# Issuing a stage's modulation weights from GpSimd, two contraction tiles in one transfer, with the bias added as a column

## The chip, the cores and the metric

The kernel runs on one core of a Trainium2 chip. The metric is the device time of one launch in microseconds, as the median of several runs. The engines are TensorE (PE, with its weight loads PEld), VectorE (DVE), ScalarE (ACT), GpSimd (POOL) and SyncE (SP, which only issues transfers). Each engine works through its own instructions in order and waits on semaphores for the others.

## The reference

A backbone of two layers works on 256 latent tokens and 256 context tokens of width 2048. Each layer first turns the conditioning vector into six modulation rows of 2048 values (shift, scale and gate of the mixer, then shift, scale and gate of the feed-forward part):

```python
sh1, sc1, g1, sh2, sc2, g2 = jnp.split(jax.nn.silu(c) @ ada_w[l] + ada_b[l], 6, axis=-1)
h = modulate(x_lat, norm_mix[l], sh1, sc1)
...
y, yc = even_mixer(h, hc, ...)        # layer 0: gated DeltaNet heads beside neighbourhood attention
y = shortconv_mixer(h, ...)           # layer 1
...
x_lat = x_lat + g1[:, None, :] * y
x_lat = x_lat + g2[:, None, :] * swiglu(modulate(x_lat, norm_ffn[l], sh2, sc2), ...)
```

Here `modulate` is an RMS norm with a learned gain, times one plus the scale, plus the shift. All values are float32. `ada_w[l]` is 2048 x 12288, so each modulation row of 2048 values costs a read of 16 MB of weights.

## The kernel before

**Matrix products.** The large products split each weight tile into a high and a low part (`split_w`: ScalarE writes `whi`, VectorE writes `wlo` at L250) and each takes three matmuls. The weights come as 512 KB tiles `raw` that SyncE issues at L236, with four buffers in the mixer's part. `fm_stream` (matmuls at L348) leaves features on the partitions, `tm_stream` (L303, L304, L308, L320) leaves tokens there.

**The mixer of layer 0.** After the projections of the DeltaNet keys, queries and values come, in this order, the attention's keys and values (`C_KB`, `C_VB`, two halves each), its queries in two halves with the attention heads between them (`na_scores`, `na_values`), the gate `C_ZA`, and the output product `ev_w_out` in two halves. The recurrence of the DeltaNet heads is laid between the steps of these streams (`plan`). Near the end of the value projection seven loads of 512 KB bring back the latent half of the inputs (`hC`, L1276); these are the only transfers that GpSimd issues. GpSimd also clears the tiles `xd` and `xdT` (L1053, L1054) and copies blocks (L1006). In the attention each head loads its position bias `bq` (L1307) and its keys and values from SyncE.

**The modulation of the mixer's stage.** Three modulation rows of layer 0 are needed only after the mixer: the gate of the mixer (`seg` 2, kept as a row) and the shift and scale of the feed-forward part (`seg` 3 and 4, kept as columns). They are not made by matmuls but by VectorE, in `ada_mixer`, which cuts them into 12 blocks of 512 columns. For a block, VectorE clears an accumulator `acc` of 128 x 512 (L430), SyncE loads the 512 bias values into its first partition (L431), and for each of the 16 contraction tiles `k` SyncE loads a tile `araw` of 128 x 512 values, 256 KB (L433), and VectorE multiplies it with the column `cT[:, k]` and adds it to the accumulator (`total`, L438). `close` then sums `acc` over the partitions with four small matmuls against ones (L445) and `ada_done` writes the four resulting columns: with the gain for a scale (L358), as a copy otherwise (L360).

There are six buffers `araw` (`AB`) and the loads run six tiles ahead (`AHEAD`): right after `total(i)` the load of tile i + 6 is issued, into the buffer that this sum has just freed. A block is closed `LAG` steps after its last sum. `Pump` draws the 192 steps along with the steps of the streams: 1.6 per step in the attention's keys and values, 0.6 in its queries, 2.0 in the gate and the output product; what is left is drawn at the end of the output product. A sum is tied behind the last written `wlo` (`last_lo`).

**The order.** The program is written in a certain order, and a planner that simulates the engines (`schedule_with_timeline_sim=True`) places each instruction on its engine's queue. Where SyncE's and GpSimd's transfers stand in their queues is so decided ahead of the run; at run time each queue keeps its order.

**Start.** At the start ScalarE loads the biases of the first two modulation rows as `brow`, 32 rows of 128, and a transpose makes the columns `bT` of them (L661). A tile `pad_e` of 48 columns keeps the layout of the memory.

Of the kernel before, what the change touches and what calls it, by code (L numbers as in the profile page):

```python
# [23 lines left out]
F32 = mybir.dt.float32  # L24
F32R = mybir.dt.float32r
AF = mybir.ActivationFunctionType
OP = mybir.AluOpType
AX = mybir.AxisListType

D = 2048  # L30
# [15 lines left out]
AB = 6  # L46
AHEAD = 6
# [65 lines left out]
def body(tc, x, c, ctx, c_ctx, ada_w, ada_b, norm_mix, norm_ffn, ffn_w_gate, ffn_w_up, ffn_w_down,  # L113
# [3 lines left out]
    PE, ACT, DVE, POOL, SP = nc.tensor, nc.scalar, nc.vector, nc.gpsimd, nc.sync  # L117
# [23 lines left out]
    def pool(name, bufs=1, stack=root, **kw):  # L141
        if kw.get("space") is not bass.MemoryType.DRAM:
            kw.setdefault("reuse_waits", "tile")
        p = stack.enter_context(tc.tile_pool(name=name, bufs=bufs, **kw))
        return p if "space" in kw else Rows(p)
# [3 lines left out]
    epool = pool("even")  # L149
# [11 lines left out]
    def smt():  # L161
        small.append(small.pop(0))
        return small[0].tile([128, 512], F32, name="sm", tag="sm")
# [11 lines left out]
    def acopy(dst, src):  # L175
        ACT.activation(dst, src, AF.Copy)  # L176
# [8 lines left out]
    def C(n):  # L185
        o, w = CO[n]
        return cs[:, o:o + w]
# [5 lines left out]
    def transpose(dst, src):  # L193
        n = src.shape[0]
        return PE.transpose(dst, src, ident[:n, :n])  # L195

    cT = cpool.tile([128, 32], F32, name="cT")
# [4 lines left out]
    shc = {}  # L202
    scc = {}
    gcol = {}
# [147 lines left out]
            yield  # L352


    def ada_done(l, seg, kind, gamma, fs_, p):

        if kind == "sc":
            DVE.scalar_tensor_tensor(scc[l, seg - 1][:, fs_], p, 1.0, gamma[:, fs_], op0=OP.add, op1=OP.mult)  # L358
        else:
            DVE.tensor_copy((shc if kind == "sh" else gcol)[l, seg][:, fs_], p)  # L360
# [3 lines left out]
    def ada_job(pool_, l, seg, kind, gamma=None):  # L364
# [5 lines left out]
        def close(acc, blk):  # L370
            fs_ = slice(blk * 8, (blk + 1) * 8)
            at = pool_.tile([128, 32, 32], F32, name="accT", tag="accT", bufs=1)
            ar = pool_.tile([128, 8, 4], F32, name="accR", tag="accR", bufs=1)
            DVE.transpose(at.rearrange("p b r -> p (b r)"), acc)
            for _ in range(LATER):
                yield
            DVE.tensor_reduce(ar.rearrange("p k b -> p (k b)"), at, axis=AX.X, op=OP.add)
            for _ in range(LATER):
                yield
            p = smt()  # L380
            for b in range(4):
                PE.matmul(p[b * 32:b * 32 + 32, 0:8], C("fold"), ar[:, :, b], start=True, stop=True)
            if kind == "row":
                gc = pool_.tile([128, 8], F32, name="gcol8", tag="gcol8", bufs=1)
                acopy(gc, p[:, 0:8])
                pc = smt()
                transpose(pc[0:8, 0:128], gc)
                g = pool_.tile([16, 128], F32, name="grow", tag="grow", bufs=1)[0:8]
                acopy(g, pc[0:8, 0:128])
                ACT.dma_start(row_d[l, seg][fs_], g)  # L390
            else:
                ada_done(l, seg, kind, gamma, fs_, p[:, 0:8])
# [22 lines left out]
    def ada_mixer(pool_, parts):  # L415


        wr = ada_w[0].rearrange("(k p) n -> p k n", p=128)
        blocks = [(seg, kind, gamma, b) for seg, kind, gamma in parts for b in range(4)]
        accs, raws = {}, {}  # L420

        def load(i):
            n, k = divmod(i, KT)
            if n >= len(blocks):
                return
            seg, b = blocks[n][0], blocks[n][3]
            c0 = seg * D + b * 512
            if not k:
                acc = accs[n] = pool_.tile([128, 512], F32, name="acc", tag="acc", bufs=2)
                DVE.memset(acc, 0.0)  # L430
                SP.dma_start(acc[0:1, :], ada_b[0:1, c0:c0 + 512])  # L431
            raws[i] = pool_.tile([128, 512], F32, name="araw", tag="araw", bufs=AB)
            SP.dma_start(raws[i], wr[:, k, c0:c0 + 512])  # L433

        def total(i):
            n, k = divmod(i, KT)
            with tc.issue_after(last_lo[0]):
                DVE.scalar_tensor_tensor(accs[n], raws.pop(i), cT[:, k:k + 1], accs[n], op0=OP.mult, op1=OP.add)  # L438

        def close(n):  # L440
            seg, kind, gamma, b = blocks[n]
            acc = accs.pop(n)
            p = smt()
            for f in range(4):
                PE.matmul(p[:, f:f + 1], acc[:, f * 128:(f + 1) * 128], ones[:, 0:1], start=True, stop=True)  # L445
            ada_done(0, seg, kind, gamma, slice(b * 4, b * 4 + 4), p[:, 0:4])
            if kind == "row" and b == 3:
                p = smt()
                transpose(p[0:16, 0:128], gcol[0, seg])
                g = pool_.tile([16, 128], F32, name="grow", tag="araw", bufs=AB)  # L450
                DVE.tensor_copy(g, p[0:16, 0:128])
                SP.dma_start(row_d[0, seg], g)

        for i in range(AHEAD):
            load(i)
        N = len(blocks) * KT
        for i in range(N + LAG):
            if i < N:
                total(i)
                load(i + AHEAD)  # L460
            if i >= KT + LAG - 1 and (i - LAG + 1) % KT == 0:
                close((i - LAG + 1) // KT - 1)
            yield
# [77 lines left out]
    sp = pool("start", stack=st, side="right")  # L541
# [15 lines left out]
    p = smt()  # L557
# [7 lines left out]
    ACT.dma_start(vrow[0:32, :], norm_mix.rearrange("l (k p) -> (l k) p", p=128))  # L565
    ACT.dma_start(vrow[32:64, :], norm_ffn.rearrange("l (k p) -> (l k) p", p=128))
    ACT.dma_start(vrow[64:112, :], od_conv.rearrange("o t (k p) -> (o t k) p", p=128))
    brow = sp.tile([32, 128], F32, name="brow")
    bT = sp.tile([128, 32], F32, name="bT")
    ACT.dma_start(brow, ada_b[0:1, 0:4096].rearrange("o (r p) -> (o r) p", p=128))  # L570
    ACT.dma_start(erow, ev_conv.rearrange("o t (k p) -> (o t k) p", p=128))
    ACT.dma_start(cs[:, 128:NCST], cst[:, 128:NCST])
    g_mix = [vecT[:, l * 16:(l + 1) * 16] for l in range(2)]
# [77 lines left out]
    def columns():  # L651

        p = smt()
        transpose(p[:, 0:112], vrow)
        DVE.tensor_copy(vecT, p[:, 0:112])
        p = smt()
        transpose(p[:, 0:120], erow)
        DVE.tensor_copy(evcT, p[:, 0:120])
        p = smt()
        transpose(p[:, 0:32], brow)  # L660
        DVE.tensor_copy(bT, p[:, 0:32])  # L661

    acopy(pick, C("pick"))
    alog = epool.tile([128, 16], F32, name="alog")
    dtb = epool.tile([128, 16], F32, name="dtb")
    gnb = epool.tile([128, 128], F32, name="gnb")


    scale = HD ** -0.5
# [100 lines left out]
    def qa_evac(q):  # L770
# [12 lines left out]
        return head_evac(2, q, 16, done, True)  # L783

    columns()
    with tc.issue_after(token_features()):
        firsts = [split_w(load_w([(wv, C_KA, 512)], 0, 2)), split_w(load_w([(wv, C_KA + 512, 256)], 0, 4))]
# [15 lines left out]
    for b in range(8):  # L803
# [4 lines left out]
        p = smt()  # L808
# [29 lines left out]


    pump = Pump([ada_mixer(adap, [(2, "row", None), (3, "sh", None), (4, "sc", g_ffn[0])])], 1, 1)  # L840

    drive(fm_stream([(wv, C_KA + 768, 256)], ks, [0, 1], lambda f, p: ka[1](f + 2, p)), every=2)
# [28 lines left out]
    eg = epool.tile([128, 3, 2, 4, 8], F32, name="eg")  # L871
    negegc = epool.tile(gsh, F32, name="negegc")
    brest = epool.tile(gsh, F32, name="brest")
    epool.tile([128, 48], F32, name="pad_e")

    def gates():
        w = abp
# [522 lines left out]
    def norm_row(t):  # L1400

        DVE.tensor_reduce(ss2[:, t:t + 1], ssx[:, t, :], axis=AX.X, op=OP.add)
        return rstd(rpool, ss2[:, t:t + 1], [128, 1], 1, D, f"nx{t}")
# [222 lines left out]
    for half in range(2):  # L1626
        c0 = half * 1024
# [7 lines left out]
        for f in range(8):  # L1635
            k = half * 8 + f
            p = smt()
# [25 lines left out]
    for t in range(2):  # L1663
        r = norm_row(t)
# [37 lines left out]
```

## Time and profile before

| | |
|---|---|
| time before, median of 3 runs | 2723.41 us (2722.6 to 2723.89) |
| the profiled execution's own time | 2726.88 us |
| its span, from the first to the last instruction | 2725.1 us |
| transfers moved | 682.71 MB, mean 251 GB/s |
| of these by GpSimd's queue (q0) | 1904 packets, 3.67 MB |
| mean granted clock of TensorE | 0.992 |

The profile is of one execution. Busy times say how long an engine had an instruction in work. A window row gives its length, then for each engine its busy time and its number of instructions, then the granted clock of TensorE as a share of full speed, the mean busy share of the 16 DMA engines and the GB/s that they moved. In a timeline row the last bracket is the idle time of the engine ahead of the instruction and what ended it. Engines marked with q (SPq, POOLq) are the issuing queues of an engine.

### The profile page before, as it was taken

The numbers are of one execution on the slowest core, as the hardware profiler recorded it, in microseconds if no ns is written. First come the engines' busy times: TensorE is split into PE (matmuls) and PEld (weight loads), VectorE is DVE, ScalarE is ACT, GpSimd is POOL, SyncE is SP. The second block draws the span as 40 slices with busy tenths as digits, with TensorE's granted clock in tenths as the row PEclk, the third lists the DMA queues.
The fourth block names the chain that finished last, engine by engine and source line by source line (L and its number), as shares of the span: only waits on it lengthen the run. The fifth ranks groups of instructions, "written<-read, shape, count | busy, mean of one in ns | idle before, by whom it ended". The sixth has DMA issues, their size and how long they took to land.

```text
span 2725.1 us, 37531 instructions
## 1 busy us (share of the span) xinstructions
PE 2655.1 (97%) x13775; PEld 2188.7 (80%) x13775; DVE 1923.7 (71%) x2652; ACT 1279.2 (47%) x1851; POOL 47.1 (2%) x73
## 2 busy tenths in 40 slices
PE   6999999999989999999999999999999999999998
PEld 4688888787877888888888878888878888888886
DVE  3378798856678877776788878888575555545675
ACT  3257633244454544444455554444464444445554
POOL 0000101100000000000000000000000000000000
PEclk9999999999999999999999999999999999999999
DMA  9945587986657878888888859997577777666653
GB/s 368 349 156 178 177 278 241 319 266 178 224 220 255 320 274 296 293 300 271 299 282 284 295 161 344 317 337 273 178 234 237 225 239 225 216 195 218 195 193 110
DMA packets 285124, 682.71 MB, mean 251 GB/s; under 512 B 56969, under 2 KB 98545, under 8 KB 283531
## 3 DMA queue, kind: packets, MB, share of 16 engines
q1 hardware_dynamic: 278660, 667.16, 73.1%
q10 hardware_dynamic: 4375, 9.48, 1.0%
q0 software_dynamic: 1904, 3.67, 0.4%
q8 instruction: 108, 1.77, 0.3%
q14 instruction: 77, 0.63, 0.1%
HBM read 658.16 MB, written 22.05 MB: 250 GB/s over the span
## 4 chain that ended last, share of the span: by engine, by line
PE 91%; DMA 3%; DVE 2%; ACT 2%; issue 1%; SPq 1%; DVEq 0%; ACTq 0%
PE mm L303 22%; PE mm L308 21%; PE mm L304 21%; PE mm L348 10%; PE mm L320 8%; PE sm L195 2%; PE sm L599 1%; PE gd L348 1%; DMA bq<-in_ev_rpb_dram 1%; DMA araw<-in_ada_w_dram 1%; PE sm L1337 1%; PE gd L1143 0%; PE gd L942 0%; DMA xn<-in_ctx_dram 0%; DVE wlo L250 0%
## 5 line engine op out<-in xcount | busy, mean ns | idle before, releaser
L250 DVE TENSOR_TENSOR wlo<-raw,whi 128x1024 fp32r<-128x1024 f32 x800 | 971.3, 1221 | 447.9 <-ACT whi L176 437.6
L176 ACT ACTIVATE whi<-raw 128x1024 fp32r<-128x1024 f32 x800 | 843.5, 1062 | 864.2 <-PE mm L308 636.2
L303 PE MATMUL mm<-whi,fhi 128*128 128x512 f32 x1232 | 482.3, 393 | 2.6 <-DVE fhi L1459 2.6
L304 PE MATMUL mm<-wlo,fhi 128*128 128x512 f32 x1232 | 479.8, 390 | 0.5 <-DVE wlo L250 0.5
L308 PE MATMUL mm<-whi,flo 128*128 128x512 f32 x1232 | 389.9, 390 | 0.0
L403 DVE SCALAR_TENSOR_TENSOR acc<-araw,cT,acc 128x1024 f32<-128x1024 f32 x224 | 286.5, 1279 | 37.6 <-DMA araw<-in_ada_w_dram 34.5
L303 PEld LDWEIGHTS mm<-whi,fhi 128*128 128x128 f32 x1232 | 231.6, 188 | 51.2 <-DVE fhi L1459 4.2
L308 PEld LDWEIGHTS mm<-whi,flo 128*128 128x128 f32 x1232 | 231.1, 188 | 48.4
L304 PEld LDWEIGHTS mm<-wlo,fhi 128*128 128x128 f32 x1232 | 231.5, 188 | 47.4 <-DVE wlo L250 0.9
L303 PE MATMUL mm<-whi,ahi 128*128 128x512 f32 x664 | 259.1, 390 | 0.0
L304 PE MATMUL mm<-wlo,ahi 128*128 128x512 f32 x664 | 258.3, 389 | 0.0
L348 PE MATMUL mm<-hB,whi 128*128 128x512 f32 (+1 forms) x840 | 235.3, 366 | 1.0 <-DVE hB L623 1.0
L308 PE MATMUL mm<-whi,alo 128*128 128x512 f32 x664 | 206.6, 389 | 0.0
L348 PEld LDWEIGHTS mm<-hB,whi 128*128 128x128 f32 x840 | 147.7, 189 | 24.3 <-DVE hB L623 2.2
L179 ACT ACTIVATE ahi<-prodT 128x256 fp32r<-128x256 f32 x176 | 73.1, 418 | 182.9 <-PE mm L304 178.1
L438 DVE SCALAR_TENSOR_TENSOR acc<-araw,cT,acc 128x512 f32<-128x512 f32 x192 | 142.4, 745 | 12.2 <-DMA araw<-in_ada_w_dram 10.9
L348 PE MATMUL mm<-hB,wlo 128*128 128x512 f32 (+1 forms) x420 | 149.5, 364 | 0.0
L308 PEld LDWEIGHTS mm<-whi,alo 128*128 128x128 f32 x664 | 124.6, 188 | 26.0
L303 PEld LDWEIGHTS mm<-whi,ahi 128*128 128x128 f32 x664 | 124.7, 188 | 25.7
L304 PEld LDWEIGHTS mm<-wlo,ahi 128*128 128x128 f32 x664 | 124.7, 188 | 25.5
L303 PE MATMUL mm<-whi,dhi 128*128 128x512 f32 x336 | 131.2, 393 | 1.2 <-DVE dhi L1459 1.2
L304 PE MATMUL mm<-wlo,dhi 128*128 128x512 f32 x336 | 130.8, 390 | 0.0
(422 smaller groups left out, 3530.3 us busy)
## 6 DMA issues: line engine op xcount, KB each, us to landing
araw<-in_ada_w_dram SPq DMA_DIRECT2D x288, 512.0 KB
raw<-in_ffn_w_down_dram SPq DMA_DIRECT2D x176, 512.0 KB
raw<-in_ffn_w_gate_dram SPq DMA_DIRECT2D x160, 512.0 KB
raw<-in_ffn_w_up_dram SPq DMA_DIRECT2D x160, 512.0 KB
raw<-in_ev_w_in_dram SPq DMA_DIRECT2D x112, 512.0 KB
araw<-in_ada_w_dram SPq DMA_DIRECT2D x192, 256.0 KB
raw<-in_od_w_in_dram SPq DMA_DIRECT2D x96, 512.0 KB
raw<-in_ev_w_out_dram SPq DMA_DIRECT2D x32, 512.0 KB
```

Source lines behind the costliest of these rows:

```text
L176: ACT.activation(dst, src, AF.Copy)
L179: ACT.activation(hi, src, AF.Copy)
L195: return PE.transpose(dst, src, ident[:n, :n])
L250: last_lo[0] = DVE.tensor_tensor(lo, raw, hi, op=OP.subtract).ins
L303: PE.matmul(ps[ti][n], a, hi[:, n * 512:(n + 1) * 512], start=first, stop=False)
L304: ins = PE.matmul(ps[ti][n], a, lo[:, n * 512:(n + 1) * 512], start=False, stop=False).ins
L308: last_mm[0] = PE.matmul(ps[ti][n], b, hi[:, n * 512:(n + 1) * 512], start=False, stop=False).ins
L320: ins = PE.matmul(ps[ti][n], a(t), w[:, c_], start=False, stop=a is ll and hi is group[-1][0]).ins
L348: last_mm[0] = PE.matmul(o, wt, h_(slice(0, len(ws)), mv, k), start=i == 0 and g == 0 and j == 0, stop=i == len(ks) - 1 and g == len(group ...
L403: DVE.scalar_tensor_tensor(acc, raw, cT[:, k:k + 1], acc, op0=OP.mult, op1=OP.add)
L438: DVE.scalar_tensor_tensor(accs[n], raws.pop(i), cT[:, k:k + 1], accs[n], op0=OP.mult, op1=OP.add)
L599: ins = PE.matmul(pr[32 * j:32 * j + 32, :], cT2[:, g + j, :], raw[:, j].rearrange("p s n -> p (s n)"), start=g == 0, stop=g == KT - 4).ins
```

## The change

GpSimd issues the weights of `ada_mixer`, and each transfer brings two contraction tiles (512 KB) into one of three buffers of twice the size; the load that follows `total(i)` is that of tile i + 4, and only every second one issues. The accumulator is no longer cleared and no bias is loaded into it: the first sum of a block is a product with a scalar. The biases of these three rows come with `brow` (80 rows in place of 32) and are kept as 48 columns `bM`, which take the place of `pad_e`; `ada_done` adds them.

```diff
-    def ada_done(l, seg, kind, gamma, fs_, p):
-
-        if kind == "sc":
+    def ada_done(l, seg, kind, gamma, fs_, p, bias=None):
+
+        if bias is not None:
+            dst = scc[l, seg - 1] if kind == "sc" else (shc if kind == "sh" else gcol)[l, seg]
+            DVE.tensor_tensor(dst[:, fs_], p, bias, op=OP.add)
+            if kind == "sc":
+                DVE.scalar_tensor_tensor(dst[:, fs_], dst[:, fs_], 1.0, gamma[:, fs_], op0=OP.add, op1=OP.mult)
+        elif kind == "sc":
...
             if not k:
-                acc = accs[n] = pool_.tile([128, 512], F32, name="acc", tag="acc", bufs=2)
-                DVE.memset(acc, 0.0)
-                SP.dma_start(acc[0:1, :], ada_b[0:1, c0:c0 + 512])
-            raws[i] = pool_.tile([128, 512], F32, name="araw", tag="araw", bufs=AB)
-            SP.dma_start(raws[i], wr[:, k, c0:c0 + 512])
+                accs[n] = pool_.tile([128, 512], F32, name="acc", tag="acc", bufs=2)
+            if k % 2:
+                return
+            raw = pool_.tile([128, 2, 512], F32, name="araw", tag="araw", bufs=AB // 2)
+            POOL.dma_start(raw, wr[:, k:k + 2, c0:c0 + 512])
+            for j in range(2):
+                raws[i + j] = raw[:, j, :]
...
             with tc.issue_after(last_lo[0]):
-                DVE.scalar_tensor_tensor(accs[n], raws.pop(i), cT[:, k:k + 1], accs[n], op0=OP.mult, op1=OP.add)
+                if k:
+                    DVE.scalar_tensor_tensor(accs[n], raws.pop(i), cT[:, k:k + 1], accs[n], op0=OP.mult, op1=OP.add)
+                else:
+                    DVE.tensor_scalar(accs[n], raws.pop(i), cT[:, 0:1], None, op0=OP.mult)
...
-            ada_done(0, seg, kind, gamma, slice(b * 4, b * 4 + 4), p[:, 0:4])
+            m0 = (seg - 2) * 16 + b * 4
+            ada_done(0, seg, kind, gamma, slice(b * 4, b * 4 + 4), p[:, 0:4], bM[:, m0:m0 + 4])
...
-                g = pool_.tile([16, 128], F32, name="grow", tag="araw", bufs=AB)
+                g = pool_.tile([16, 128], F32, name="grow", tag="araw", bufs=AB // 2)
...
             if i < N:
                 total(i)
-                load(i + AHEAD)
+                if i:
+                    load(i + AHEAD - 2)
...
-    brow = sp.tile([32, 128], F32, name="brow")
+    brow = sp.tile([80, 128], F32, name="brow")
     bT = sp.tile([128, 32], F32, name="bT")
-    ACT.dma_start(brow, ada_b[0:1, 0:4096].rearrange("o (r p) -> (o r) p", p=128))
+    ACT.dma_start(brow, ada_b[0:1, 0:5 * D].rearrange("o (r p) -> (o r) p", p=128))
...
-        transpose(p[:, 0:32], brow)
+        transpose(p[:, 0:80], brow)
         DVE.tensor_copy(bT, p[:, 0:32])
+        DVE.tensor_copy(bM, p[:, 32:80])
...
+    bM = epool.tile([128, 48], F32, name="bM")
...
-    epool.tile([128, 48], F32, name="pad_e")
```

## The prediction

> **What bounds the kernel now.** I read the page first, then the busy time by stretches of the stage that the change touches, then TensorE's timeline for the gaps in it, then the chain that ended last.
>
> ```profile
> span 2725.1 us, 37531 instructions
> PE 2655.1 (97%) x13775; PEld 2188.7 (80%) x13775; DVE 1923.7 (71%) x2652; ACT 1279.2 (47%) x1851; POOL 47.1 (2%) x73
> L438 DVE SCALAR_TENSOR_TENSOR acc<-araw,cT,acc x192: 623/746/754, 329.3 to 868.2; 128x512 f32<-128x512 f32 x192
> 320.00:540.00 220.00, 217.62 (x1520) 180.61 (x1519) 190.02 (x360) 74.31 (x113) 17.96 (x28) 0.99 0.85 272
> 540.00:600.00 60.00, 53.76 (x373) 50.38 (x372) 36.12 (x68) 22.36 (x45) 3.49 (x3) 0.94 0.90 279
> 600.00:660.00 60.00, 54.93 (x817) 48.28 (x817) 37.12 (x75) 27.41 (x56) 2.76 (x2) 0.97 0.71 197
> 740.00:790.00 50.00, 41.63 (x227) 34.62 (x228) 35.09 (x87) 31.02 (x82) 0.00 (x0) 0.93 0.48 167
> 857.00:880.00 23.00, 19.38 (x78) 15.52 (x77) 18.29 (x41) 7.02 (x17) 0.00 (x0) 0.85 0.46 165
> ```
>
> TensorE is busy 97% of the span, so only its gaps can be won. The changed work (the sums of L438) runs from 329.3 to 868.2 us. In the windows the columns are length, then busy time of PE, PEld, DVE, ACT and POOL, then granted clock, DMA share and GB/s. From 320 to 540 TensorE idles 220.00 - 217.62 = 2.4 us; from 540 to 660 it idles 6.2 + 5.1 = 11.3 us, and the clock there (0.94 and 0.97) costs another 3.6 + 1.8 = 5.4 us; from 740 to 790 it idles 8.4 and from 857 to 880 3.6 us. The gaps, by what ended them:
>
> ```profile
> 571.76 0.39 PE L348 MATMUL mm<-hC,wlo 128*128 128x256 f32 x1 [4.36 <-DVE wlo L250]
> 581.74 1.65 PE L1143 MATMUL gd<-vtok,xdT 128*128 128x128 f32 x8 [1.88 <-DMA vtok<-vd__151]
> 639.71 3.26 PE L1337 MATMUL sm<-PT,vb 128*128 128x256 f32 x8 [3.72 <-DVE PT L173]
> 869.03 1.87 PE L445 MATMUL sm<-cs,acc 128*128 128x1 f32 x8 [3.24 <-DVE acc L438]
> ...
> 560.97 8.95 DMA bq<-in_ev_rpb_dram
> 571.85 9.85 DMA vtok<-vd__151
> 627.10 7.58 DMA bq<-in_ev_rpb_dram
> ```
>
> The chain (start, length, what) puts a load ahead of each of the first three: VectorE runs in order, so while it waits for bq the split wlo stands behind it and TensorE starves. These loads are issued by SyncE, as are the modulation weights. The stretch from 740 to 790 is, by the code, the end of the GDN heads' recurrence, which the change doesn't touch.
>
> **The change part by part.** The prices, from the views of the tiles and the groups by line (the tiles' rows give least, median and longest in ns, and first and last start):
>
> ```profile
> L433 SPq DMA_DIRECT2D araw<-in_ada_w_dram x192: 327/328/2325, 140.2 to 860.6; - x192
> L431 SPq DMA_DIRECT2D acc<-in_ada_b_dram x12: 251/262/1157, 143.4 to 825.3; - x12
> L430 DVE MEMSET acc<- x12: 485/485/485, 141.5 to 824.8; 128x512 f32 x12
> L438 DVE SCALAR_TENSOR_TENSOR acc<-araw,cT,acc 128x512 f32<-128x512 f32 x192 | 142.4, 745 | 12.2 <-DMA araw<-in_ada_w_dram 10.9
> L1322 DVE TENSOR_SCALAR s<-s,l 128x512 f32<-128x512 f32 x16 | 7.6, 482 | 0.4
> L614 DVE TENSOR_TENSOR sh<-sm,bT x8: 149/151/151, 36.1 to 136.6; 128x4 f32<-128x4 f32 x8
> L661 DVE COPY bT<-sm x1: 191/191/191, 11.9 to 11.9; 128x32 f32<-128x32 f32 x1
> L1276 POOL DMA_DIRECT2D hC<-h_d x7: 713/713/830, 527.7 to 542.3; - x7
> ```
>
> *VectorE.* Twelve clears go: 12 x 0.485 = 5.8 us. The first of each sixteen sums becomes a product with a scalar, which L1322 has in the same shape at 0.482: 12 x (0.745 - 0.482) = 3.2 us. Added: in the four scale blocks one operation on four columns (L614: 0.151), 0.6 us; in the eight others an addition takes the place of a copy, taken as equal. One copy of 48 columns at the start (L661: 0.19 for 32) is not used before the sums that begin at 329.3, and stands beside the copy of bT at 11.9, far ahead of bT's first reader at 36.1; taken as 0, at most 0.2. Net 8.2 us of VectorE. On the path counts what falls where TensorE idles, 13.7 of the 340 us from 320 to 660, 4%: **-0.3 us**; all of it would be -8.2.
>
> *SyncE.* 192 issues of 0.328 and 12 of 0.262 leave it, 66 us in all, with their waits for VectorE to free a buffer. The first six, from 140.2 us, are needed at 329.3 only: their place is worth nothing. What counts is the issue time ahead of the late loads (SyncE's timeline: start, length):
>
> ```profile
> 546.54 0.60 SPq L433 DMA_DIRECT2D araw<-in_ada_w_dram  x1
> 551.25 1.16 SPq L431 DMA_DIRECT2D acc<-in_ada_b_dram  x1
> 553.95 0.38 SPq L433 DMA_DIRECT2D araw<-in_ada_w_dram  x1
> 560.22 1.38 SPq L1307 DMA_DIRECT2D bq<-in_ev_rpb_dram  x2
> 562.35 0.42 SPq L433 DMA_DIRECT2D araw<-in_ada_w_dram  x1
> 567.46 0.83 SPq L433 DMA_DIRECT2D araw<-in_ada_w_dram  x1
> 617.13 0.85 SPq L433 DMA_DIRECT2D araw<-in_ada_w_dram  x2
> 625.49 0.38 SPq L433 DMA_DIRECT2D araw<-in_ada_w_dram  x1
> 626.44 1.48 SPq L1307 DMA_DIRECT2D bq<-in_ev_rpb_dram  x2
> ```
>
> Ahead of the first bq stand 0.60 + 1.16 + 0.38 = 2.1 us, between it and vtok 1.25, ahead of the later bq 1.23: together 4.6 us, if SyncE had nothing else to wait for. At the other end nothing is won, since bq itself needs 7.6 to 9.0 us to land and its buffer may be what held it. I take half, 2.3, and with it the clock that idling costs (5.4 us for 11.3 us of idling, 0.48 for each): **-3.4 us**. Late next is the landing of bq, which stays.
>
> The Trainium skill, page "DMA: Bandwidth & Descriptors", section "Issuing engines are not separate DMA queues", says that transfers of all issuers share the same 16 engines and another issuer saves only issue time. The trace agrees so far as a DMA share of 0.90 from 540 to 600 leaves little room; by that rule this term can't pass the issue time, and the sum stays.
>
> *GpSimd.* 96 issues of 0.713 us (hC has the same size and shape) are 68 us on an engine that is busy 47.1. They stand in its order among the clears of xd and xdT and the seven hC loads; behind a load that waits for VectorE these stand too, and nobody on TensorE has waited for them so far.
>
> *The shorter lead.* Before, each sum freed one of six buffers and its reload had six sums of time. Now the second sum of a pair frees one of three pairs, which is first needed after four further sums.
>
> ```profile
> DMA to landing us min/median/max: 6.0/7.8/11.4
> 527.70 2.25 POOL L1276 DMA_DIRECT2D hC<-h_d  x3 [21.08 <-PE mm L308]
> 534.03 0.72 POOL L1276 DMA_DIRECT2D hC<-h_d  x1 [4.07 <-issue]
> 360.00:400.00 40.00, 19.78 (x27) 1.00 0.93 314
> 800.00:840.00 40.00, 19.98 (x28) 1.00 0.92 328
> 360.00:400.00 40.00, 40.00 (x190) 33.34 (x189) 37.36 (x72) 9.72 (x11) 1.81 (x1) 1.00 0.93 314
> 800.00:840.00 40.00, 40.00 (x182) 33.20 (x181) 38.54 (x50) 18.25 (x24) 0.00 (x0) 1.00 0.92 328
> ```
>
> The first two window rows are L438 alone, the last two all work. A pair's buffer goes round in 0.71 issue + landing + 2 x 0.745 for its sums, and three pairs give six sums in that time. With hC's landings (first row) that is 8.2, 10.0 or 13.6 us, so 1.37, 1.67 or 2.27 us for a sum. Wanted are 40/27 = 1.48 and 40/28 = 1.43. At 6.0 us nothing waits. At 7.8 VectorE waits 27 x 0.19 + 28 x 0.24 = 11.7 us, less its idle 2.6 + 1.5: +7.6 us, and the split wlo stands behind each wait. At 11.4 for every pair it would be about +41. GpSimd seems to hold three transfers in flight (three at once, the fourth when the first has landed); hC had all three against SyncE's queue, a pair will have one or two beside it, so I stay near 6.0: a quarter of 7.6, **+1.9 us**. The last pair ahead of L445 at 869.03 is in this term.
>
> The Trainium skill, same page, section "Anatomy of one DMA — SWDGE (gpsimd) path", gives 2.0 us + bytes/436e3 for such a transfer, an estimate of 3.2 us here; by it this term is 0 and the sum -3.7. The trace's 7.8 under load decides.
>
> **The sum:** -0.3 - 3.4 + 1.9 = -1.8 us. Against the profiled execution, 2726.88 us (the span and 1.8 around it), that is 2725.1; the profile is 3.5 above the median of the runs, 2723.41, so I carry the difference: **2721.6 us**, own range 2717 to 2727.
>
> **The rivals.**
>
> *SyncE's relief is worth much more.* Two thirds of the gaps of 4.36, 1.88 and 3.72 close with their clock: 9.96 x 1.48 x 2/3 = 9.8 us, 2713.6. For it: weight issues of L433 stand close ahead of each of these loads, and one lasts up to 2.3 us where 0.33 is the least. Against: bq's landing alone is longer than the gaps, and from 320 to 540 TensorE has 2.4 us to give.
>
> *Pairs come late* (slower). The price above with 7.8 us landings and nothing won on SyncE: +7.6 - 0.3, 2730.7. It decides once a pair takes over some 6.5 us to land in the dense stretches. For it: VectorE already waited 10.9 us for these weights with six sums of lead. Against: fewer transfers in flight than hC had.
>
> *GpSimd's order holds the loads back.* From 527.7 to 542.3 its queue issues hC, after 21.08 us of waiting. Loads behind that have a lead of five sums at 539/192 = 2.8 us, 14 us; they'd be late by 0.6 us if only the issuing blocks them, by 22 if the waiting does too. I take +6: 2727.6.
>
> *VectorE's work stretches the issue.* The row of hC shows at most 830 against 713 ns, in a stretch in which VectorE is busy 190 of 220 us, so little speaks for it. Were each load held for one whole operation like L1322's (0.48 us), a sum in the dense stretches took 0.08 us more, 55 x 0.08 = 4.4 us on top of late pairs: 2735. The Trainium skill, page "SBUF — State Buffer", section "Who interferes with whom", says that such a VectorE operation in its fast mode shuts GpSimd out of a shared port until it ends; it speaks against this change.
>
> *Nothing is relieved*, since SyncE merely waits elsewhere: 2723.
>
> **How the numbers follow.** Forecast 0.42, relief 0.30, late pairs 0.16, GpSimd's order 0.07, stretched issue 0.03, nothing 0.02. A measurement of this kernel tells about 0.2%, 5.4 us, from no change: below 2718.0 is faster, above 2728.8 slower. Faster: relief and 0.04 of the forecast, 0.34. Slower: late pairs, stretched issue and 0.04 of GpSimd's order, 0.23. Same: 0.43. The range 2710 to 2732 cuts off the far parts of relief (0.06), late pairs (0.08) and GpSimd's order (0.02) and all of the stretched issue, 0.19.
>
> **What would show it.** VectorE: no clears of acc, twelve products near 0.48 us. SyncE: bq issued 1 to 2 us earlier against the matmuls beside it, gaps at L348 and L1337 shorter by about that. Lead: waits of L438 for araw near 10.9 us or little over; 20 or more speak for late pairs, and a landing row for araw near 6 us against them. I am wrong if the stretch from 320 to 540, where TensorE has 2.4 us to give, changes by more than that in either direction: then the planner's new order, which no row here shows, did it.

## The result, and the profile after

The changed kernel takes 2746.77 us (median of 4 runs, 2744.08 to 2750.62) against 2723.01 us (2721.72 to 2723.89) for the kernel before, measured beside it. The ratio is 1.0089 with a 95% interval of 1.0077 to 1.0101: slower by some 24 us, where 1.8 us faster had been forecast, and beyond the upper end of the predicted range (2732).

The profiled execution of the changed kernel took 2748.94 us. The first fence is its page: the span, the busy times, and the group of the sums by line (busy time and mean of one, then VectorE's idle time ahead of them and what ended it).

```profile
span 2747.2 us, 37272 instructions
...
PE 2659.1 (97%) x13775; PEld 2191.5 (80%) x13775; DVE 1915.8 (70%) x2645; ACT 1279.1 (47%) x1851; POOL 117.2 (4%) x169
...
L446 DVE SCALAR_TENSOR_TENSOR acc<-araw,cT,acc 128x512 f32<-128x512 f32 x180 | 134.3, 747 | 23.3 <-DMA araw<-in_ada_w_dram 22.2
```

TensorE is busy 4.0 us more than before (2655.1) in a span that is 22.1 us longer: some 18 us are new gaps, and the other 4 us are longer busy times of the same matmuls, beside a mean granted clock of 0.988 against 0.992. VectorE's busy time fell by 7.9 us (1923.7 before), close to the 8.2 that the removed work comes to, and still the kernel is slower. Its waits for weights ahead of the sums doubled, from 10.9 us to 22.2.

The view of the tile `araw` of the changed kernel (count, then least, median and longest in ns):

```profile
L438 POOL DMA_DIRECT2D araw<-in_ada_w_dram x96: 722/722/841, 131.4 to 880.8; - x96
...
L448 DVE TENSOR_SCALAR acc<-araw,cT x12: 478/481/487, 328.5 to 861.9; 128x512 f32<-128x512 f32 x12
...
DMA to landing us min/median/max: 3.9/6.2/11.2
```

The issues (0.722 us) and the first sums (0.481 us) cost what the prediction priced them at, and a pair's median landing of 6.2 us is the value that it had taken as nearly harmless. The same windows as before, in the changed kernel:

```profile
320.00:540.00 220.00, 207.66 (x1432) 171.90 (x1431) 180.94 (x349) 70.89 (x105) 49.88 (x71) 0.97 0.81 255
540.00:600.00 60.00, 55.52 (x402) 51.33 (x401) 32.30 (x63) 20.33 (x40) 11.90 (x15) 0.97 0.90 274
600.00:660.00 60.00, 47.88 (x698) 41.75 (x697) 32.23 (x63) 22.20 (x48) 6.38 (x7) 0.88 0.71 202
```

TensorE's busy time in the first window fell from 217.62 to 207.66 us. It had 2.4 us of idling there and now has 12.3, and in the third window the idling went from 5.1 to 12.1 us while the clock fell from 0.97 to 0.88. Between them, from 540 to 600 us, TensorE idles less than before (4.5 us against 6.2). To see where the delay arises, take the start of the n-th weight split `wlo`, counted from 0 over the whole program, in the profiled execution of each version (the versions come below):

| n-th split, its start before | 64, 428.3 us | 80, 544.6 us | 92, 614.2 us | 100, 679.2 us | 799, 2696.8 us |
|---|---|---|---|---|---|
| changed kernel | +4.3 | +8.9 | +19.8 | +24.8 | +22.3 |
| pairs by SyncE | +0.8 | +3.1 | +13.8 | +16.6 | +12.8 |
| single tiles by GpSimd | +2.2 | +7.8 | +14.0 | +20.7 | +18.3 |
| single tiles by SyncE, new bias | -1.0 | -5.2 | +5.3 | +2.8 | +0.2 |

The full loss of the changed kernel is there at split 100 and doesn't grow behind it, so it arises between about 400 and 680 us, where the DeltaNet recurrence lies beside the streams. The columns between are rougher, since the versions lay the recurrence differently among the streams: the base version is 5.2 us ahead at split 80 and 5.3 behind at split 92, and ends level. TensorE's timeline of the changed kernel shows the gaps there (start, length, instruction, idle time ahead of it and what ended it):

```profile
420.71 1.65 PE L955 MATMUL gd<-cs,gm 128*128 128x128 f32 x6 [6.30 <-DVE nt L1000]
...
514.92 0.28 PE L1098 MATMUL gd<-xd,n 32*32 32x32 f32 x2 [5.08 <-DMA xd<-dz]
...
607.40 1.19 PE L1156 MATMUL gd<-R,xdT 128*128 128x128 f32 x4 [4.07 <-ACT qst L1276]
...
636.98 1.08 PE L1111 MATMUL gd<-Y,xdT 32*32 32x32 f32 x64 [5.62 <-DVE state L1169]
```

The chain of waits says what stood ahead of each of the four (start, length, what):

```profile
409.39 9.08 DMA dz<-lsol
...
507.36 7.43 DMA xd<-dz
...
594.72 9.46 DMA raw<-in_ev_w_in_dram
...
624.24 9.21 DMA bq<-in_ev_rpb_dram
```

None of the four is a transfer that the change touches. They are the recurrence's blocks, the projection's weights and the attention's bias, all of them issued by SyncE, and they take 7.4 to 9.5 us to land. The length alone isn't new: two of the chain's loads of `bq` took 8.95 and 7.58 us before. `dz<-lsol` took 6.67 us there and 9.08 here.

### The profile page after: what moved, and what is told of

The parts are those of the page before. It is cut to its first block, busy times and chain, and to the rows that moved or that the text cites. A ratio compares the mean times of both kernels' runs of the same rounds, so it can differ in the third digit from the quotient of the medians.

```text
span 2747.2 us, 37272 instructions
## 1 busy us (share of the span) xinstructions
PE 2659.1 (97%) x13775; PEld 2191.5 (80%) x13775; DVE 1915.8 (70%) x2645; ACT 1279.1 (47%) x1851; POOL 117.2 (4%) x169
## 4 chain that ended last, share of the span: by engine, by line
PE 87%; DMA 5%; DVE 3%; ACT 2%; issue 2%; SPq 1%; POOL 0%; ACTq 0%; DVEq 0%; POOLq 0%
PE mm L303 21%; PE mm L308 21%; PE mm L304 21%; PE mm L348 9%; PE mm L320 7%; PE sm L195 2%; DMA araw<-in_ada_w_dram 2%; DMA bq<-in_ev_rpb_dram 1%; PE sm L611 1%; PE gd L348 1%; DVE wlo L250 1%; PE sm L1350 1%; PE gd L955 1%; DMA xd<-dz 1%; DVE acc L446 0%
## 5 line engine op out<-in xcount | busy, mean ns | idle before, releaser
L348 PE MATMUL mm<-hB,whi 128*128 128x512 f32 (+1 forms) x840 | 234.6, 366 | 1.0 <-DVE hB L635 1.0
L348 PEld LDWEIGHTS mm<-hB,whi 128*128 128x128 f32 x840 | 147.7, 189 | 24.3 <-DVE hB L635 2.3
L446 DVE SCALAR_TENSOR_TENSOR acc<-araw,cT,acc 128x512 f32<-128x512 f32 x180 | 134.3, 747 | 23.3 <-DMA araw<-in_ada_w_dram 22.2
L348 PE MATMUL mm<-hB,wlo 128*128 128x512 f32 (+1 forms) x420 | 149.7, 365 | 0.0
```

Source lines behind the costliest of these rows:

```text
L348: last_mm[0] = PE.matmul(o, wt, h_(slice(0, len(ws)), mv, k), start=i == 0 and g == 0 and j == 0, stop=i == len(ks) - 1 and g == len(group ...
```

## The experiments

Three theories went into the runs. *Pairs*: two tiles in one transfer and three buffers bring the weights late. *Issuer*: something about GpSimd as the issuer costs the time, either its order or a second stream of transfers beside SyncE's. *Order*: any edit makes the planner order the program anew, and that alone moves the time. Every kernel below was made from the changed one or from the first of these versions; distances are medians against the kernel before as measured beside that version, intervals are 95% and belong to the ratio.

### The bias and the clears alone

```diff
-            if k % 2:
-                return
-            raw = pool_.tile([128, 2, 512], F32, name="araw", tag="araw", bufs=AB // 2)
-            POOL.dma_start(raw, wr[:, k:k + 2, c0:c0 + 512])
...
+            raws[i] = pool_.tile([128, 512], F32, name="araw", tag="araw", bufs=AB)
+            SP.dma_start(raws[i], wr[:, k, c0:c0 + 512])
...
-                if i:
-                    load(i + AHEAD - 2)
+                load(i + AHEAD)
```

> The bias column and the dropped clears alone: SyncE issues single tiles with six buffers as before. Theory A (pairs in three buffers come late), theory B (weights issued by GpSimd: its order, and a second stream beside SyncE's loads) both expect no loss, 2718 to 2724 us. Theory C (the planner's new order of all queues, which any edit here brings) expects a loss of its own here, over 5 us either way.

Measured: 2723.65 us, +1.4; ratio 1.0006 (0.9997 to 1.0015). VectorE is relieved and the time doesn't move. The order of the program did change (the matmuls of the recurrence stand elsewhere among those of the streams), so a new order by itself need not cost anything. This version, with single tiles in six buffers issued by SyncE, is the base of what follows.

### Pairs by SyncE, and single tiles by GpSimd

```diff
-            POOL.dma_start(raw, wr[:, k:k + 2, c0:c0 + 512])
+            SP.dma_start(raw, wr[:, k:k + 2, c0:c0 + 512])
```

> As the changed kernel, but SyncE issues the pairs. Theory A: most of the loss stays, 2738 to 2748 us, and L446 waits 20 us or more for araw. Theory B: near the kernel before, 2720 to 2728.

Measured: 2738.76 us, +16.5; ratio 1.0053 (1.0036 to 1.0070).

The other half alone is the base version with the issuer changed:

```diff
-            SP.dma_start(raws[i], wr[:, k, c0:c0 + 512])
+            POOL.dma_start(raws[i], wr[:, k, c0:c0 + 512])
```

> As the changed kernel, but GpSimd issues single tiles of 256 KB into six buffers, six ahead. Theory A: the loss is gone, 2718 to 2728 us. Theory B: it stays or grows, since GpSimd now issues 192 transfers, 2740 or more.

Measured: 2737.52 us, +15.3; ratio 1.0059 (1.0042 to 1.0075). Each half alone costs some 15 us, both together 24. By these times there are two causes, which overlap in part.

### Is it GpSimd's order behind hC?

In both versions by GpSimd the longest wait of VectorE for weights lay behind the seven `hC` loads. This is GpSimd's timeline in the changed kernel:

```profile
540.67 1.57 POOL L1289 DMA_DIRECT2D hC<-h_d  x2 [2.19 <-PE mm L308]
...
554.15 0.71 POOL L1289 DMA_DIRECT2D hC<-h_d  x1 [4.16 <-issue]
555.53 0.73 POOL L438 DMA_DIRECT2D araw<-in_ada_w_dram  x1 [0.67 <-issue]
557.50 0.73 POOL L438 DMA_DIRECT2D araw<-in_ada_w_dram  x1 [1.24 <-DVE R L1139]
563.34 0.73 POOL L438 DMA_DIRECT2D araw<-in_ada_w_dram  x1 [5.11 <-issue]
```

From the first `hC` to 555.53 us, 14.9 us, no weights are issued, and the load at 563.34 stands another 5.11 us for nothing that the profile names. It looks like the cause, so these loads were given to SyncE, once in the changed kernel and once with single tiles:

```diff
-            POOL.dma_start(raw, wr[:, k:k + 2, c0:c0 + 512])
+            (SP if 102 <= i < 110 else POOL).dma_start(raw, wr[:, k:k + 2, c0:c0 + 512])
```

> The changed kernel, but the four pairs that stood behind the seven hC loads in GpSimd's order (102 to 109) are issued by SyncE. Theory 'GpSimd's order' (the loads stand behind hC, and the whole loss of GpSimd as issuer comes from there): VectorE's wait of 8.0 us for araw near 563 is gone, and 10 to 15 us come back: 2732 to 2737. Theory 'lead and stream' (two transfers less ahead, and a second stream beside SyncE's loads all along 400 to 660): the 8.0 us wait is gone, but only 0 to 5 us come back, 2742 to 2747, since the gaps at 420, 515 and 637 lie elsewhere.

> Single tiles by GpSimd, with six buffers, but the eight tiles behind hC (102 to 109) by SyncE. Theory 'GpSimd's order': near the kernel before, 2722 to 2728, since the loss of 15 us arose from 540 to 565 in that kernel's trace. Theory 'second stream': 2734 to 2738, as with all tiles on GpSimd (2737.5).

Measured: the changed kernel with that edit 2748.92 us, +28.1; ratio 1.0096 (1.0081 to 1.0111). Single tiles 2739.93 us, +19.1; ratio 1.0062 (1.0044 to 1.0081). Nothing came back. In the version with single tiles the recurrence stands among the streams exactly as without this edit, so no new order hides a gain there. The waits did go; VectorE's view of waits from 330 to 680 us, in the version with single tiles (total, times, longest):

```profile
DVE bq L1317 <- DMA bq<-in_ev_rpb_dram: 25.2, 5, 6.5
...
DVE nt L995 <- DMA dz<-lsol: 8.1, 1, 8.1
...
DVE sub_tmp L1037 <- DMA lsol<-dl: 5.8, 1, 5.8
...
DVE acc L442 <- DMA araw<-in_ada_w_dram: 2.7, 1, 2.7
```

The same view of the kernel before:

```profile
DVE acc L438 <- DMA araw<-in_ada_w_dram: 10.8, 12, 5.1
...
DVE nt L987 <- DMA dz<-lsol: 4.4, 1, 4.4
```

VectorE waits only 2.7 us for the weights in this stretch, less than the 10.8 in the kernel before, and still the kernel is 19 us slower. The waits that grew are those for `dz` and `lsol`, the recurrence's own blocks. TensorE's longest gap in that version, and the chain ahead of it:

```profile
588.19 0.58 PE L348 MATMUL mm<-hC,wlo 128*128 128x256 f32 x1 [9.80 <-DVE wlo L250]
```

```profile
574.90 11.45 DMA bq<-in_ev_rpb_dram
...
586.92 1.23 DVE wlo L250
```

One of the two transfers of a head's bias, 96 KB issued by SyncE, took 11.45 us from issue to landing; VectorE waited for it, the split `wlo` stood behind, and TensorE starved.

### Is it the second stream?

If the weights in GpSimd's queue take bandwidth from what SyncE has issued, then less of them must help, although the issues, the waits for buffers and the sums stay as many. The diff is that of the version by GpSimd; the one by SyncE differs from it in the issuer alone. (In both, the small tile `grow` of the last step gets a buffer of its own.)

```diff
-            raws[i] = pool_.tile([128, 512], F32, name="araw", tag="araw", bufs=AB)
-            POOL.dma_start(raws[i], wr[:, k, c0:c0 + 512])
+            raws[i] = pool_.tile([128, 256], F32, name="araw", tag="araw", bufs=AB)
+            POOL.dma_start(raws[i], wr[:, k, c0:c0 + 256])
...
+            raw = raws.pop(i)[:, None, :].to_broadcast([128, 2, 256])
...
```

> Single tiles by SyncE, but each load brings only the left half of its columns (128 KB) and the sum reads that half twice: half of the weights is left out, so half of their bytes, while issues, sums and buffers stay as many. The control for the kernel with the same loads by GpSimd. Both theories: at or below 2723.7, perhaps 5 to 10 us below, since the stretch from 480 to 600 has a DMA share of 0.9 and more.

> The same half loads by GpSimd. Theory 'second stream' (the weights of GpSimd's queue take bandwidth from the loads in SyncE's queue, which land later): with half of the bytes the distance to SyncE's version shrinks from 14 us to 7 or less. Theory 'GpSimd's issuing' (its order, its waits, its 0.54 us for an issue): the distance stays 12 us or more.

Measured: by SyncE 2725.67 us, +4.0; ratio 1.0009 (0.9999 to 1.0018). By GpSimd 2724.84 us, +3.2; ratio 1.0011 (1.0001 to 1.0020). The distance between the two issuers, 14 us with whole tiles, is gone. GpSimd's issues stayed as many and as long:

```profile
L436 POOL DMA_DIRECT2D araw<-in_ada_w_dram x192: 539/539/1147, 136.8 to 856.0; - x192
```

So that many issues of this length need not cost anything. That the bytes cost the 14 us is likely but not shown, since the planner's order moved too (a table below gives by how much). That SyncE's version gained nothing from half of the bytes was a miss of both theories: halving these weights' bytes under SyncE's issue frees nothing. VectorE's waits in the half version by GpSimd:

```profile
DVE acc L444 <- DMA araw<-in_ada_w_dram: 12.2, 2, 10.4
...
DVE nt L997 <- DMA dz<-lsol: 6.1, 1, 6.1
...
DVE sub_tmp L1039 <- DMA lsol<-dl: 3.0, 1, 3.0
```

The wait of 10.4 us behind `hC` is still there, and costs nothing to speak of. The waits for the recurrence's own blocks are shorter, 6.1 and 3.0 us against 8.1 and 5.8 in the fence above. The landing of the load itself is not the price, though: on the chain of waits `dz<-lsol` took 10.01 us with single tiles by GpSimd and still 8.53 us in this half version. The base version by SyncE has 6.1 us for `dz`, and for `lsol` (the second fence, from the view of that tile from 380 to 680 us) 1.5:

```profile
DVE wlo L250 <- ACT whi L176: 14.1, 14, 1.8
DVE nt L995 <- DMA dz<-lsol: 6.1, 1, 6.1
...
DVE acc L442 <- DMA araw<-in_ada_w_dram: 3.0, 7, 0.6
```

```profile
  DMA lsol<-dl: 1.5, 1
```

Is it GpSimd, or any issuer but SyncE?

```diff
-            SP.dma_start(raws[i], wr[:, k, c0:c0 + 512])
+            ACT.dma_start(raws[i], wr[:, k, c0:c0 + 512])
```

> Single tiles in six buffers, all by ScalarE in place of SyncE or GpSimd. Theory 'second stream': 2734 to 2742, as with GpSimd, since the weights again aren't in the queue of SyncE's small loads. Theory 'GpSimd's issuing': 2721 to 2728; if ScalarE's own work is held up by these issues (192 of some 0.3 to 0.7 us), more, and then the trace has to show VectorE's waits for ScalarE longer than the 14 us of whi in the version by SyncE.

Measured: 2731.21 us, +9.6; ratio 1.0037 (1.0024 to 1.0050). It is between the two expectations, so it decides less than hoped. VectorE's waits in that version:

```profile
DVE wlo L250 <- ACT whi L176: 18.9, 16, 7.2
DVE nt L995 <- DMA dz<-lsol: 7.4, 1, 7.4
...
DVE sub_tmp L1037 <- DMA lsol<-dl: 5.7, 1, 5.7
```

The recurrence's blocks come late as with GpSimd (7.4 and 5.7 us), which speaks for the second stream; ScalarE's own work is held up too (7.2 us at the longest), which the base version had at 1.8, so part of the 9.6 us can be that.

### Where GpSimd may issue

```diff
-            POOL.dma_start(raws[i], wr[:, k, c0:c0 + 512])
+            (SP if 40 <= i < 128 else POOL).dma_start(raws[i], wr[:, k, c0:c0 + 512])
```

> Single tiles: by SyncE for sums 40 to 127 (about 385 to 680 us, the recurrence beside the attention), by GpSimd before and behind. Theory 'second stream': 2721 to 2727, since outside of that stretch no small load of SyncE ends on TensorE's path. If the loss stays at 10 us or more, it doesn't come from the stretch in which the trace shows it, but from the order that the planner makes of a program with loads on GpSimd.

Measured: 2723.49 us, +1.9; ratio 1.0006 (0.9996 to 1.0017). More than half of the weights are issued by GpSimd here, 104 of 192, and it costs nothing; it gains nothing either. TensorE's order is that of the base version but for a few places, so this shows GpSimd's issue outside of the recurrence's stretch to be free. What the issuer costs belongs to that stretch.

### The pairs: their lead or their size

> Pairs issued by SyncE in three buffers, but each pair by two transfers of 256 KB, one behind the other. Theory 'lead' (a pair's buffer comes free later than a single tile's, so the weights arrive late): as with one transfer of 512 KB, 2736 to 2740. Theory 'size' (one transfer of 512 KB lands later as a whole and holds up the 64 KB loads of xd, xdT and lsol, which took 5.0, 6.0 and 6.6 us to land beside pairs and 2.6, 3.7 and 3.4 beside single tiles): most of the 15 us comes back, 2723 to 2728.

The edit, on pairs by SyncE:

```diff
-            SP.dma_start(raw, wr[:, k:k + 2, c0:c0 + 512])
             for j in range(2):
+                SP.dma_start(raw[:, j, :], wr[:, k + j, c0:c0 + 512])
                 raws[i + j] = raw[:, j, :]
```

Measured: 2730.85 us, +10.0; ratio 1.0035 (1.0024 to 1.0047). It fell between the theories again: with the pairs' lead but transfers of 256 KB, most of the cost stays. The remaining distance to whole pairs, 0.18%, is no more than the two intervals leave uncertain, so the cost of the size isn't shown by the times.

The lead without any pair, single tiles by SyncE:

```diff
-AB = 6
-AHEAD = 6
+AB = 4
+AHEAD = 4
```

> Single tiles by SyncE, bias as a column, but four buffers in place of six. Theory 'lead': VectorE's waits for araw rise above 20 us and the time goes to 2735 or more. Theory 'size': the waits rise, but the small loads land as early as with six buffers, and the time stays within 2722 to 2730.

Measured: 2736.95 us, +16.1; ratio 1.0058 (1.0040 to 1.0077). Two buffers less cost what the pairs cost. VectorE's waits for the weights rose, from 3.0 us in the base version to 20.0 (330 to 680 us), just short of the more than 20 that the theory of the lead had named:

```profile
DVE acc L442 <- DMA araw<-in_ada_w_dram: 17.5, 19, 2.6
...
DVE acc L444 <- DMA araw<-in_ada_w_dram: 2.5, 3, 1.2
```

That VectorE's waits are the way to TensorE isn't borne out, though. With pairs by SyncE they are, over the same stretch:

```profile
DVE acc L446 <- DMA araw<-in_ada_w_dram: 8.4, 8, 1.7
...
DVE acc L448 <- DMA araw<-in_ada_w_dram: 2.2, 3, 1.6
```

This is 10.6 us, as much as in the kernel before, and the kernel loses 16.5 us. Its two longest gaps on TensorE lie elsewhere:

```profile
627.71 0.49 PE L1105 MATMUL gd<-xdT,Y 32*32 32x32 f32 x21 [8.01 <-DVE state L1169]
```

```profile
509.80 0.24 PE L1098 MATMUL gd<-xd,n 32*32 32x32 f32 x2 [5.10 <-DMA xd<-dz]
```

VectorE's timeline shows what held `state` up in the first:

```profile
625.87 0.56 DVE L1322 TENSOR_TENSOR bq<-bq,cs 128x384 f32<-128x384 f32 x1 [8.89 <-DMA bq<-in_ev_rpb_dram]
626.34 1.12 DVE L1169 SCALAR_TENSOR_TENSOR state<-state,eg,gd 128x128 f32<-128x128 f32 x4
```

Both are again small loads of SyncE. (The chain of waits names a pair's landing ahead of this `state`; the timeline shows that VectorE stood at `bq`, so that step of the chain is a guess of the view.) The landings of `xd<-dz`, 64 KB each, first in the base version, then beside whole pairs (the traces have only two of sixteen in each, so this is a hint and no more):

```profile
DMA to landing us min/median/max: 2.0/2.6/3.3
```

```profile
DMA to landing us min/median/max: 4.3/5.0/5.7
```

So the cost of the shorter lead is shown by the times, and its path only in part: the two longest gaps end at small loads, and that these land later rests on few records.

### Both causes put together

The changed kernel, with SyncE issuing the pairs of sums 40 to 127:

```diff
-            POOL.dma_start(raw, wr[:, k:k + 2, c0:c0 + 512])
+            (SP if 40 <= i < 128 else POOL).dma_start(raw, wr[:, k:k + 2, c0:c0 + 512])
```

> The changed kernel, but SyncE issues the pairs of sums 40 to 127 (about 385 to 680 us), GpSimd those before and behind. Theory 'two causes' (the pairs' short lead and size cost about 15 us in that stretch whoever issues them, the second stream the rest): 2736 to 2740, the time of the version with all pairs by SyncE, with GpSimd's issue outside the stretch costing nothing. If GpSimd's issue cost it all: 2722 to 2728. If the pairs cost it all and the issuer nothing: 2745 to 2750, as the changed kernel.

Measured: 2738.05 us, +16.8; ratio 1.0062 (1.0046 to 1.0079). That is the time of all pairs by SyncE. So of the 24 us some 16 to 17 are the pairs', whoever issues them, and the rest, some 7, is what GpSimd's issue adds to them in the recurrence's stretch (ratio 1.0089, at least 1.0077, against 1.0053, at most 1.0070, with all pairs by SyncE); with single tiles it costs 15. No version with all of its weights beats the kernel before; the ones that equal it keep single tiles in six buffers, and SyncE as the issuer beside the recurrence.

How far the planner's order moved can be counted in the traces. The recurrence has 1768 matmuls that write `gd` (those of L348 left out), and the streams 10720 that write `mm`. For each matmul of the recurrence I count the stream matmuls ahead of it; the table gives by how many this differs between two versions, as a mean over the 1768.

| two versions, with their distances from the kernel before | mean shift |
|---|---|
| pairs by SyncE (+16.5), both causes put together (+16.8) | 0.0 |
| base (+1.4), GpSimd outside of the recurrence (+1.9) | 0.2 |
| pairs by SyncE as two transfers (+10.0), changed kernel (+23.8) | 0.9 |
| pairs by SyncE (+16.5), changed kernel (+23.8) | 1.6 |
| base (+1.4), pairs by SyncE (+16.5) | 1.7 |
| base (+1.4), four single buffers (+16.1) | 7.4 |
| base (+1.4), single tiles by GpSimd (+15.3) | 14.8 |
| base (+1.4), single tiles by ScalarE (+9.6) | 24.1 |
| kernel before, base (+1.4) | 28.1 |
| single tiles by GpSimd (+15.3), the same in halves (+3.2) | 28.5 |

A stream matmul takes 0.36 us on average from 400 to 680 us in the kernel before, so a shift of 1.7 is an estimated 0.6 us. The pairs' 15 us and the 7 us that GpSimd's issue adds to them come with nearly the same order, so they are hardly the order's. For single tiles by GpSimd or ScalarE, and for the half loads, the order moved some eight times as far or more, so there the issuer and the bytes aren't separated from it; that an order can move so far for nothing is seen in the base version.

## Why the prediction was wrong

*VectorE, -0.3 us: not contradicted.* The removed work shows in the busy time and not in the time: the base version gives +1.4 us, interval about -1 to +4, too wide to see 0.3. (The items of the sum give 8.4 us of removed work, or 8.2 with the most that the copy at the start can cost.)

*SyncE, -3.4 us: the step that failed in its sign.* It counted only the issue time that leaves SyncE ahead of `bq` and `vtok`, if SyncE had nothing else to wait for. With every issue taken from SyncE and the lead kept, the kernel is 15.3 us slower; with pairs, and nearly the same order, it is 7 us slower than with SyncE issuing beside the recurrence. SyncE's timeline of the changed kernel has the first `bq` at 572.37 us, 12.2 us later than the 560.22 of before:

```profile
554.79 12.41 SPq L236 DMA_DIRECT2D raw<-in_ev_w_in_dram  x2
...
572.37 0.94 SPq L1320 DMA_DIRECT2D bq<-in_ev_rpb_dram  x1
```

The first row shows that its condition didn't hold. With no weights to issue, SyncE stands at the second of two loads `raw`, 11.6 us by its view of waits, until VectorE's split frees a buffer, and the small loads stand behind it. VectorE in turn had waited 7.98 us, until 564.92, for the weights behind `hC`. The planner's order around this `bq` differs from before, so the 1 to 2 us that were to show can't be read against the work beside it. The three gaps that were to close did go: TensorE's view of waits from 320 to 680 us has none for `wlo`, `vtok` or `PT` any more. Five others, of 3.9 to 6.3 us, took their place.

The step also left out that the weights then form a second stream beside the loads of SyncE. The half loads fit this, and as many issues of the same length cost nothing there, but the mechanism stays open: that a weight issued behind a small load in SyncE's own queue doesn't slow it, and one from another queue does, is how I read this, and no run tested it by itself. The prediction had the DMA share of 0.90 in hand and read it as a limit of the gain only. The Trainium skill, page "DMA: Bandwidth & Descriptors", section "Issuing engines are not separate DMA queues", says that transfers of all issuers share 16 engines. Its conclusion, that another issuer saves issue time only, holds here in so far as nothing more was gained; that the kernel can lose 7 us by it with pairs, and 15 with single tiles, is what these runs add.

*The shorter lead, +1.9 us: the largest error. The mechanism was named, its size was wrong.* With whole pairs by SyncE it is 16.5 us, with four single buffers 16.1, outside even the 7.6 that 7.8 us landings would have given, though inside the far bound of 41. The landing was near the one taken (6.2 us against 6.0); the fault is in the unit. The step priced VectorE's waits for the weights, and these have no fixed price: 10.8 us of them before and 12.2 in the half version by GpSimd cost next to nothing, while with 10.6 in pairs by SyncE 16.5 us are lost, and with 2.7 in one version by GpSimd 19.1. At the longest gaps of these versions it is small loads that TensorE waits for, by way of VectorE or directly.

*The rivals.* In number the stretched issue came nearest (2735), as an addition to late pairs (2730.7); late pairs was the nearest that the runs bear out, and too cheap for the same reason. GpSimd's order behind `hC` was the most plausible story in the trace, and fell: without it nothing comes back. A stretched issue fell too: the longest of 96 took 0.841 us against 0.722. (With single tiles one of 192 took 1.204 against 0.537.) The rival that would have reached the result, a second stream that slows the loads of SyncE, wasn't among them.

*The signs.* VectorE's waits of 22.2 us spoke for late pairs and the landing of 6.2 us against them, so the two signs contradict each other and decide nothing; the runs did. The window from 320 to 540 us lost 10.0 us of TensorE's work, far over the 2.4 named, but the reading given for it, the planner's new order, isn't borne out: the base and both half versions have orders of their own and stay within 0.11% of the kernel before, and pairs by SyncE lose 15 us in nearly the order of the base.

*What stays open.* No run was built to hold the planner's order. It happened to stay nearly the same for the pairs, but not for single tiles by GpSimd or ScalarE nor for the half loads, so how much of their 15 and 9.6 us is a second stream and how much an order that is worse for the recurrence isn't separated; the shift counts TensorE's order alone. Nor is it shown why a shorter lead delays the small loads, or whether they land later or are issued later.

## What to carry to other kernels

When a stream of large loads moves to another issuer, price not the issue time that it saves but the small, urgent loads that stay behind: here, with the DMA engines 0.7 to 0.9 busy, the move cost 7 us with pairs and 15 with single tiles, where 3.4 were hoped for. Look also at what the relieved queue will wait for next. A total of an engine's waits isn't a price: look at the longest gaps of the engine that bounds the kernel, and at which load stands ahead of each. Two tiles in one transfer halve the issues but also take lead from the prefetch; with room for six tiles, four ahead was worse than six by 0.5%.

## What the runs showed of the hardware

GpSimd's issue time goes with the shape of the transfer and not with its bytes alone. A single tile of 256 KB, in the version with single tiles by GpSimd, took 0.537 us against 0.722 for a pair, which has two rows of 512 values for each partition; half a tile, 128 KB, took 0.539, as shown above:

```profile
L436 POOL DMA_DIRECT2D araw<-in_ada_w_dram x192: 537/537/1204, 132.8 to 874.8; - x192
```

SyncE took 0.328 us for a tile and 0.368 for a pair, as the view of `araw` in the last version shows:

```profile
L438 SPq DMA_DIRECT2D araw<-in_ada_w_dram x44: 367/368/1653, 399.7 to 670.9; - x44
```

GpSimd's queue seems to have only a few transfers in flight: behind `hC` its next issues stand 3 to 5 us with nothing to wait for that the profile names (4.16 and 5.11 us in the timeline above). That was seen, not tested by itself; it did no harm here. And halving the bytes of the weights under SyncE's issue changed nothing that can be measured, in a stretch whose DMA share in the base version is 0.85 (320 to 540 us) and 0.91 (540 to 600): a high share of the DMA engines didn't mean that bytes bound the kernel.
